# Tiles multiplied by x before its norm is known, and weight rests queued behind the norm's chain on VectorE

## The chip, the core and the metric

The kernel runs on one core of one Trainium2 chip. The metric is the device time of one execution in microseconds (us). Engines are named as the profile names them: PE is TensorE (PEld its weight loads), DVE VectorE, ACT ScalarE, POOL GpSimd and SP SyncE, whose queue issues most loads.

## What is computed

A trunk of two layers on 256 tokens of width 1024 (float32). Each layer is a mixer and a channel mixer, each behind a norm that is modulated by a conditioning vector c (adaLN):

```python
for l in range(DEPTH):
    mod = c_act @ w_ada[l] + b_ada[l]
    sh1, sc1, g1, sh2, sc2, g2 = split(mod)
    h = rmsnorm(x, ln1_g[l]) * (1.0 + sc1) + sh1
    x = x + g1 * mixer(h, ...)            # GLA branch + RWKV-7 branch, gated, then w_out
    h = rmsnorm(x, ln2_g[l]) * (1.0 + sc2) + sh2
    f = swiglu(h, w1, w3, w2) if l % 2 == 0 else moe(h, ...)   # (silu(h w1) * (h w3)) w2, or 8 experts, top 2
    x = x + g2 * f
return rmsnorm(x, lnf_g)
```

`rmsnorm(x, g)` is `x * rsqrt(mean(x*x) + 1e-6) * g`: one number for each token times a gain for each channel. Here channels lie on the partitions and tokens along the free dimension, so the norm is one row of 256 factors, the gain and the shift are one column each.

## The kernel before

All products are made from float32 values split in two: a high part (a rounded copy, written by ScalarE) and a rest (value minus copy, written by VectorE, `split`, L358 and L359). A **tile** (`project`, L374 to L385) is a 128-column piece of a weight with 8 blocks of 128 input channels; each block is three matmuls of 128x128 by 128x256 (high by high L382, high by activation's rest L383, weight's rest by high L384), so a tile is 24 products. The activations are `hh` and `hl`, both parts of the normalized input, which `norm_split` (L387 to L394) makes for each block: VectorE multiplies x by gain and norm (t, L391), ScalarE adds the shift and rounds (hh, L392), VectorE takes the rest (hl, L393).

The norm: ScalarE squares x (`stat`, L309), TensorE sums the squares over the channels (L318), VectorE takes the reciprocal root in a chain of eight tiny instructions (`rsq`, L331 to L338), TensorE spreads the two columns over all partitions (`spread`, L344).

The order of the program is: mixer 0, `ffn` (the dense feed-forward of layer 0, 22 blocks of two tiles and one second multiplication each, L1011 to L1013, then the x updates L1039), mixer 1 (first the tiles 0 and 1, whose `shift` is L571/L572, and the small projection `pap`, L585 to L587; L596 and L599 multiply the first tile's result), the experts (`moe`). Each mixer contains a substitution loop (L700/L702, 30 steps on VectorE), after which VectorE turns the result (L704 to L706: TW, TT) and TensorE takes it up (L711, L719), then four chunks (L732 to L767) follow one another.

Beside all this the adaLN weights of what comes next are multiplied: `feed` takes one 128x1024 piece (`araw`, loaded by POOL's queue, L230) and adds it into `aacc` on VectorE (L251 for the first of eight, L253 for the others); after eight pieces TensorE and VectorE finish the group (L267, L275, L278). `pace` calls `feed` once in a number of tiles, and two pieces at a time (six in the feed-forward) are loaded ahead.

The order of the instructions on PE, DVE and ACT is set by the framework's scheduler from the program; only SP's loads stand in an order written by hand in the mixers and the feed-forward. Each engine works its own queue in order.

## Time and profile before

| | |
|---|---|
| median of 3 runs | 1783.13 us (1782.68 to 1784.4) |
| the profiled execution | 1787.74 us |
| its span, first to last instruction | 1785.9 us |
| mean granted TensorE clock | 0.969 |
| busy: TensorE, VectorE, ScalarE | 1708.7, 1152.2, 830.1 us |
| HBM read | 517.84 MB, 291 GB/s over the span |

The places that the change touches lie at 369 to 391 us (mixer 0 to feed-forward), 566 to 600 us (feed-forward to mixer 1) and in mixer 1 up to its chunks (600 to 780 us); the experts run from about 910 us to the end. A busy TensorE is not TensorE at its peak: a product of 128x256 follows the one before it after 0.12 us at full clock. In the timelines the first column is the start in us, the second the duration, and what stands in brackets is the idle time before it with what ended it.

### The profile page before, as it was taken

Reading aid. Unit: us, or ns where it says so; the run is one execution under the profiler, and the core shown is the slowest. Engines: PE = TensorE matmul, PEld = TensorE weight load, DVE = VectorE, ACT = ScalarE, POOL = GpSimd, SP = SyncE. Lnnn points to the kernel's source line nnn. Section 1 sums busy time; section 2 is a strip of 40 time slices with the busy share of each in tenths; the row PEclk is TensorE's granted clock in tenths of the full one; section 3 lists DMA queues with packets and bytes.
Section 4 is the critical chain, followed back from the end, with each engine's and each line's share of the span. In section 5 each row is a group of like instructions: output and inputs, shape, how many; then the busy total and the mean of one; then the engine's idle time right before and its main releaser. Section 6 shows DMA issues by size and latency. Waiting matters only on the chain.

```text
span 1785.9 us, 29944 instructions
## 1 busy us (share of the span) xinstructions
PE 1708.7 (96%) x11887; PEld 1406.2 (79%) x11887; DVE 1152.2 (65%) x1747; ACT 830.1 (46%) x1194; POOL 57.3 (3%) x103
## 2 busy tenths in 40 slices
PE   7898999989999999899979999999999999999997
PEld 6787889989999888899977875678656886578754
DVE  3789668776665879566768961498407982289611
ACT  3643324444444643234537750477306771267501
POOL 0000000010000000000010000000000000000001
PEclk9899799999999899799979999999999999999999
DMA  8654246777764434325678989999999999999995
GB/s 342 210 184 166 97 135 241 259 263 261 266 229 153 146 140 137 123 72 189 265 288 328 346 310 421 420 421 421 418 420 421 420 421 417 421 421 420 420 421 215
DMA packets 79973, 520.92 MB, mean 292 GB/s; under 512 B 9521, under 2 KB 10161, under 8 KB 22353
## 3 DMA queue, kind: packets, MB, share of 16 engines
q1 hardware_dynamic: 67440, 476.14, 67.2%
q0 software_dynamic: 11232, 40.90, 7.0%
q8 instruction: 95, 1.56, 0.3%
q10 hardware_dynamic: 1152, 1.89, 0.3%
q14 instruction: 54, 0.43, 0.1%
HBM read 517.84 MB, written 1.05 MB: 291 GB/s over the span
## 4 chain that ended last, share of the span: by engine, by line
PE 75%; issue 12%; DVE 6%; DMA 4%; ACT 2%; POOL 0%; SPq 0%; POOLq 0%; DVEq 0%; ACTq 0%
PE pj L1316 11%; PE pj L382 6%; PE pj L383 6%; PE pj L384 6%; PE pj L1320 6%; PE pj L1321 6%; PE pj L1322 6%; PE pc L1335 5%; DMA araw<-wada 3%; PE pc L1338 3%; PE pc L1340 3%; PE pc L1339 3%; PE pg L1365 1%; DVE lo L359 1%; PE pg L1289 1%
## 5 line engine op out<-in xcount | busy, mean ns | idle before, releaser
L1100 DVE TENSOR_TENSOR lo<-raw,hi 128x1024 fp32r<-128x1024 f32 x330 | 395.5, 1221 | 85.9 <-ACT hi L1099 78.5
L1099 ACT ACTIVATE hi<-raw 128x1024 fp32r<-128x1024 f32 x330 | 347.5, 1059 | 126.8 <-PE pj L1321 82.1
L358 ACT ACTIVATE hi<-raw 128x1024 fp32r<-128x1024 f32 (+2 forms) x209 | 213.7, 1025 | 271.3 <-PE pj L383 200.1
L382 PE MATMUL pj<-hh,hi 128*128 128x256 f32 x1040 | 306.4, 296 | 5.5 <-DVE t L572 3.2
L384 PE MATMUL pj<-hh,lo 128*128 128x256 f32 x1040 | 303.0, 292 | 3.3 <-DVE lo L359 3.3
L359 DVE TENSOR_TENSOR lo<-raw,hi 128x1024 fp32r<-128x1024 f32 (+2 forms) x209 | 246.3, 1180 | 89.0 <-ACT hi L358 84.4
L383 PE MATMUL pj<-hl,hi 128*128 128x256 f32 x1040 | 302.3, 292 | 0.0
L382 PEld LDWEIGHTS pj<-hh,hi 128*128 128x128 f32 x1040 | 204.3, 197 | 13.8 <-issue 4.7
L384 PEld LDWEIGHTS pj<-hh,lo 128*128 128x128 f32 x1040 | 204.0, 196 | 5.6 <-DVE lo L359 3.9
L383 PEld LDWEIGHTS pj<-hl,hi 128*128 128x128 f32 x1040 | 203.8, 196 | 1.9 <-issue 0.3
L1316 PE MATMUL pj<-raw,xs 128*64 128x256 f32 x1792 | 201.3, 381 | 0.0
L1320 PE MATMUL pj<-hi,xh 128*128 128x512 f32 x448 | 181.5, 405 | 0.5 <-ACT hi L1099 0.5
L1322 PE MATMUL pj<-lo,xh 128*128 128x512 f32 x448 | 178.5, 398 | 1.9 <-DVE lo L1100 1.9
L1321 PE MATMUL pj<-hi,xl 128*128 128x512 f32 x448 | 177.8, 397 | 0.0
L1316 PEld LDWEIGHTS pj<-raw,xs 128*64 128x64 f32 x1792 | 125.8, 137 | 65.0 <-issue 4.7
L1360 DVE TENSOR_TENSOR late<-late,pj 128x512 f32<-128x512 f32 (+1 forms) x56 | 30.7, 549 | 207.5 <-PE pj L1316 201.0
L1322 PEld LDWEIGHTS pj<-lo,xh 128*128 128x128 f32 x448 | 84.5, 189 | 25.8 <-DVE lo L1100 5.3
L1335 PE MATMUL pc<-raw,as 128*64 128x512 f32 x448 | 102.2, 595 | 0.0
L1320 PEld LDWEIGHTS pj<-hi,xh 128*128 128x128 f32 x448 | 84.7, 189 | 21.3 <-ACT hi L1099 1.9
L1321 PEld LDWEIGHTS pj<-hi,xl 128*128 128x128 f32 x448 | 84.7, 189 | 18.7
L253 DVE SCALAR_TENSOR_TENSOR aacc<-araw,csg,aacc 128x1024 f32<-128x1024 f32 x70 | 89.6, 1280 | 12.6 <-DMA araw<-wada 11.8
L1338 PE MATMUL pc<-hi,acts 128*128 128x512 f32 x224 | 88.2, 394 | 0.0
(406 smaller groups left out, 2660.6 us busy)
## 6 DMA issues: line engine op xcount, KB each, us to landing
raw<-moe SPq DMA_DIRECT2D x333, 1024.0 KB, 18.2
raw<-win SPq DMA_DIRECT2D x43, 1024.0 KB, 5.0
araw<-wada POOLq DMA_DIRECT2D x78, 512.0 KB, 4.7
raw<-f SPq DMA_DIRECT2D x33, 1024.0 KB, 6.9
raw<-wv SPq DMA_DIRECT2D x8, 1024.0 KB, 4.9
raw<-wog SPq DMA_DIRECT2D x8, 1024.0 KB, 5.4
raw<-wad SPq DMA_DIRECT2D x6, 1024.0 KB, 8.1
raw<-wor SPq DMA_DIRECT2D x4, 1024.0 KB, 5.2
```

The lines of the kernel that those rows point to most:

```text
L358: nc.scalar.activation(hi[:, :w], src, AF.Copy)
L359: nc.vector.tensor_tensor(lo[:, :w], src, hi[:, :w].bitcast(F32), ALU.subtract)
L382: nc.tensor.matmul(o, hi[:, s], ah[:, kc, :], start=kc == 0, stop=False)
L383: nc.tensor.matmul(o, hi[:, s], al[:, kc, :], start=False, stop=False)
L384: nc.tensor.matmul(o, lo[:, s], ah[:, kc, :], start=False, stop=kc == nk - 1)
L1099: nc.scalar.activation(hi, w[:, s], AF.Copy)
L1100: eng.tensor_tensor(lo, w[:, s], hi.bitcast(F32), ALU.subtract)
L1316: nc.tensor.matmul(p[64 * n:64 * n + 64, :T], x[:, kc], hi[:, z * 512 + n * T:z * 512 + n * T + T], start=kc == 0, stop=kc == KC - 1)
L1320: nc.tensor.matmul(p, x[0][:, kc], hi[:, s], start=kc == 0, stop=False)
L1321: nc.tensor.matmul(p, x[1][:, kc], hi[:, s], start=False, stop=False)
L1322: nc.tensor.matmul(p, x[0][:, kc], lo[:, s], start=False, stop=kc == KC - 1)
L1335: nc.tensor.matmul(py[0][64 * n:64 * n + 64], act[:, a:a + CAP], hi[:, s], start=first, stop=last)
```

## The change

Four things change.

1. **Early tiles.** At the start of the feed-forward and of mixer 1 a new function `scaled` splits x times gain, without norm and shift, in two parts `xh` and `xl` (eight copies on ScalarE, eight rests on VectorE), and puts the shift behind them as two more columns. The first three tiles (`EARLY`) multiply 258 columns of it. What they give is then treated by `normed`: VectorE copies the added column out, multiplies the 256 others by the spread norm, and the column is added (in the silu's bias, in the product of the two halves, or by itself in mixer 1).
2. **The norm's row** is copied by ScalarE from PSUM to SBUF (`rs`), and `norm_split` reads it there.
3. **A fence.** `rstd` keeps the last instruction of the rsq chain; every weight rest and every `aacc` piece that the program writes after it is queued behind it on VectorE (`issue_after`).
4. **The end of the feed-forward.** The second multiplications of the last two blocks are made together at the end, in halves, each x update behind its last product.

```diff
+        with self.behind():
+            if kc == 0:
+                self.acc = self.st.tile([P, D], F32, name="aacc")
...
@@ rsq
-            nc.vector.scalar_tensor_tensor(y, t, a, y, ALU.add, ALU.mult)
+            last = nc.vector.scalar_tensor_tensor(y, t, a, y, ALU.add, ALU.mult)
+        self.chain = last.ins
@@ rstd
         y = self.rsq(self.ss[:, :2], 2, 1.0 / D, 1e-6)
+        self.fence = self.chain
...
+    def behind(self):
+
+        return self.tc.issue_after(self.fence) if self.fence else nullcontext()
@@ split
-        nc.vector.tensor_tensor(lo[:, :w], src, hi[:, :w].bitcast(F32), ALU.subtract)
+        with self.behind():
+            nc.vector.tensor_tensor(lo[:, :w], src, hi[:, :w].bitcast(F32), ALU.subtract)
@@ project
-        o = self.pj()[:, :T]
         ah, al = act
+        o = self.pj()[:, :ah.shape[-1]]
...
+    def scaled(self, gain, sh, xh, xl):
+
+        nc = self.nc
+        for d, op in ((xh, 0), (xl, 1)):
+            e = d[:, :, T:T + 2]
+            s = sh[:, :, None].to_broadcast([P, KC, 2])
+            if op:
+                nc.vector.tensor_tensor(e, s, xh[:, :, T:T + 2].bitcast(F32), ALU.subtract)
+            else:
+                nc.scalar.activation(e, s, AF.Copy)
+        for kc in range(KC):
+            g = gain[:, kc:kc + 1]
+            nc.scalar.activation(xh[:, kc, :T], self.x[:, kc, :], AF.Copy, scale=g)
+            nc.vector.scalar_tensor_tensor(xl[:, kc, :T], self.x[:, kc, :], g, xh[:, kc, :T].bitcast(F32), ALU.mult,
+                                           ALU.subtract)
+
+    def normed(self, ps, rs, tmp, col):
+
+        nc = self.nc
+        nc.vector.tensor_copy(col, ps[:, T:T + 1])
+        t = tmp()
+        nc.vector.tensor_tensor(t, ps[:, :T], rs, ALU.mult)
+        return t
...
+EARLY = 3
+LAST_F = 2
@@ mixer, l = 1
-        rs = k.rstd()
+        xh, xl = [dp.tile([P, KC, T + 2], F32R, name=n) for n in ("BK", "vt")]
+        k.scaled(gain, sh, xh, xl)
+        pre = {i: k.project(tile_of(i), (xh, xl)) for i in range(EARLY)}
+        rs = mis[:, :T]
+        nc.scalar.activation(rs, k.rstd(), AF.Copy)
         k.norm_split(range(KC), gain, sh, rs, hh, hl, t1)
@@ ffn
-        rs = k.rstd()
+        xh, xl = [dp.tile([P, KC, T + 2], F32R, name=n) for n in ("xh", "xl")]
+        k.scaled(gain, sh, xh, xl)
...
+        for i in range(EARLY):
+            pre[i] = k.project(load(i // 2)[:, i % 2 * 1024:i % 2 * 1024 + 1024], (xh, xl))
+        rs = dp.tile([P, T], F32, name="rs")
+        nc.scalar.activation(rs, k.rstd(), AF.Copy)
+        col = dp.tile([P, EARLY], F32, name="col")
         k.norm_split(range(KC), gain, sh, rs, hh, hl, t1)
...
+        k.need(l, 5)
+        ws = [k.split(w2) for _, _, w2 in pend]
+        for m0 in (0, 4):
+            each = [(p, w, m) for m in range(m0, m0 + 4) for p, w in zip(pend, ws)]
+            if m0 == 0:
+                each = [(p, w, m) for p, w in zip(pend, ws) for m in range(4)]
+            for p, w, m in each:
+                second(*p[:2], w, m)
+                if p is pend[-1]:
+                    o = acc[m // 2][:, (m % 2) * T:(m % 2) * T + T]
+                    nc.vector.scalar_tensor_tensor(k.x[:, m], o, k.mod[l][:, 40 + m:41 + m], k.x[:, m], ALU.mult, ALU.add)
```

How the scheduler puts it on the engines shows at three places. The first is VectorE at the start of the feed-forward, in the norm's chain. The kernel before (L331 to L338 is the chain, aacc the adaLN pieces, t the first step of `norm_split`):

```order
L331 TENSOR_SCALAR rsq<-pc 128x2
L253 SCALAR_TENSOR_TENSOR aacc<-araw,csg,aacc 128x1024
L334 TENSOR_SCALAR rsq<-rsq 128x2
L278 TENSOR_TENSOR mod_78<-ada,vec 128x8
L336 TENSOR_TENSOR rsq<-rsq 128x2
L337 SCALAR_TENSOR_TENSOR rsq<-rsq 128x2
L338 SCALAR_TENSOR_TENSOR rsq<-rsq 128x2
L336 TENSOR_TENSOR rsq<-rsq 128x2
L337 SCALAR_TENSOR_TENSOR rsq<-rsq 128x2
L253 SCALAR_TENSOR_TENSOR aacc<-araw,csg,aacc 128x1024
L338 SCALAR_TENSOR_TENSOR rsq<-rsq 128x2
L253 SCALAR_TENSOR_TENSOR aacc<-araw,csg,aacc 128x1024
```

The changed kernel at the same place (the chain is L332 to L339, xl the rest of x times gain, col the added column of an early tile):

```order
L332 TENSOR_SCALAR rsq<-pc 128x2
L335 TENSOR_SCALAR rsq<-rsq 128x2
L408 SCALAR_TENSOR_TENSOR xl<-x,gain_3849,xh 128x256 x4
L337 TENSOR_TENSOR rsq<-rsq 128x2
L408 SCALAR_TENSOR_TENSOR xl<-x,gain_3849,xh 128x256 x2
L338 SCALAR_TENSOR_TENSOR rsq<-rsq 128x2
L339 SCALAR_TENSOR_TENSOR rsq<-rsq 128x2
L337 TENSOR_TENSOR rsq<-rsq 128x2
L414 COPY col<-pj 128x1
L338 SCALAR_TENSOR_TENSOR rsq<-rsq 128x2
L339 SCALAR_TENSOR_TENSOR rsq<-rsq 128x2
L279 TENSOR_TENSOR mod_78<-ada,vec 128x8
```

The aacc pieces have gone behind the chain; six of the eight xl and the copy of the first tile's column now stand in it.

The second is TensorE a little later, around the fourth tile, the first one of the feed-forward that multiplies hh and hl in the change. The kernel before (pj_4024 is the fourth tile, pj_3994 the third, lo the weight's rest):

```order
L384 MATMUL pj_3994<-hh_3847,lo_3996 128x256
L382 MATMUL pj_4024<-hh_3847,hi_4025 128x256
L383 MATMUL pj_4024<-hl_3848,hi_4025 128x256
L384 MATMUL pj_4024<-hh_3847,lo_4026 128x256
L382 MATMUL pj_4024<-hh_3847,hi_4025 128x256
```

The changed kernel (pj_3945 is the third tile, pj_4056 the fourth, pj_4127 the fifth):

```order
L392 MATMUL pj_3945<-xh_3851,lo_3947 128x258
L390 MATMUL pj_4056<-hh_3847,hi_4057 128x256
L391 MATMUL pj_4056<-hl_3848,hi_4057 128x256
L390 MATMUL pj_4127<-hh_3847,hi_4128 128x256
L391 MATMUL pj_4127<-hl_3848,hi_4128 128x256
L392 MATMUL pj_4056<-hh_3847,lo_4058 128x256
L390 MATMUL pj_4056<-hh_3847,hi_4057 128x256
```

The tile before the fourth has become an early one; in both orders the third matmul of the fourth tile takes the weight's rest, and the tile's others stand behind it.

The third is VectorE at the end of mixer 1's substitution loop. The kernel before (zt and ff are the loop's two instructions, L704 turns its result):

```order
L253 SCALAR_TENSOR_TENSOR aacc<-araw,csg,aacc 128x1024
L700 TENSOR_TENSOR zt<-ff 64x84
L359 TENSOR_TENSOR lo<-raw,hi 128x1024
L702 TENSOR_TENSOR ff<-ff,zt 64x3x28
L253 SCALAR_TENSOR_TENSOR aacc<-araw,csg,aacc 128x1024
L700 TENSOR_TENSOR zt<-ff 64x58
L703 MEMSET ff 64x32
L359 TENSOR_TENSOR lo<-raw,hi 128x1024
L702 TENSOR_TENSOR ff<-ff,zt 64x2x29
L253 SCALAR_TENSOR_TENSOR aacc<-araw,csg,aacc 128x1024
```

and, up to the turn,

```order
L700 TENSOR_TENSOR zt<-ff 64x30
L359 TENSOR_TENSOR lo<-raw,hi 128x1024
L702 TENSOR_TENSOR ff<-ff,zt 64x30
L253 SCALAR_TENSOR_TENSOR aacc<-araw,csg,aacc 128x1024
L704 STREAM_TRANSPOSE TW<-ff 32x32x32
```

The changed kernel (L744 and L746 are the loop's two instructions, L748 the turn; dg belongs to the experts' router):

```order
L367 TENSOR_TENSOR lo<-raw,hi 128x1024
L744 TENSOR_TENSOR zt<-ff 64x84
L1738 TENSOR_SCALAR dg<-router,gain_9447 128x8
L746 TENSOR_TENSOR ff<-ff,zt 64x3x28
L744 TENSOR_TENSOR zt<-ff 64x58
L747 MEMSET ff 64x32
L746 TENSOR_TENSOR ff<-ff,zt 64x2x29
L744 TENSOR_TENSOR zt<-ff 64x30
L746 TENSOR_TENSOR ff<-ff,zt 64x30
L748 STREAM_TRANSPOSE TW<-ff 32x32x32
```

No aacc piece is left in the loop (six stood in it), and ten weight rests instead of 13; the pieces of that group stand before the loop. On TensorE 66 products that stood between the last L683 and L711 now come after L711.

## Rows read from the trace of the kernel before

**Rows 1.** Page, busy time of each engine (share of the span, instructions).

```profile
PE 1708.7 (96%) x11887; PEld 1406.2 (79%) x11887; DVE 1152.2 (65%) x1747; ACT 830.1 (46%) x1194; POOL 57.3 (3%) x103
```

**Rows 2.** Table of stretches around the two norms: busy us of each engine, clock, DMA.

```profile
core 0: us, PE busy (x) PEld busy (x) DVE busy (x) ACT busy (x) POOL busy (x), PEclk, DMA share, GB/s
369.20:374.60 5.40, 1.81 (x19) 1.07 (x17) 4.75 (x14) 0.80 (x2) 0.00 (x0) 0.97 0.61 235
374.60:381.20 6.60, 5.44 (x23) 5.02 (x24) 6.54 (x15) 3.63 (x8) 2.11 (x4) 0.51 0.68 210
...
540.00:566.00 26.00, 26.00 (x219) 26.00 (x218) 13.36 (x16) 11.27 (x15) 0.00 (x0) 1.00 0.24 82
...
576.00:589.60 13.60, 9.70 (x44) 9.04 (x45) 10.41 (x28) 4.86 (x12) 1.58 (x3) 0.51 0.55 187
```

**Rows 3.** Timeline of VectorE, start of the feed-forward.

```profile
370.19 0.75 DVE L251 TENSOR_SCALAR aacc<-araw,csg 128x1024 f32<-128x1024 f32 x1 [0.45 <-PE ada L267]
...
374.43 0.15 DVE L338 SCALAR_TENSOR_TENSOR rsq<-rsq 128x2 f32<-128x2 f32 x1
...
377.08 1.27 DVE L393 SCALAR_TENSOR_TENSOR hl<-t,mod,hh 128x256 fp32r<-128x256 f32 x3
...
386.05 1.23 DVE L359 TENSOR_TENSOR lo<-raw,hi 128x1024 fp32r<-128x1024 f32 x1
```

**Rows 4.** Timeline of TensorE, the same stretch.

```profile
374.64 1.22 PE L344 MATMUL pc<-cst,rsq 128*128 128x128 f32 x4 [3.51 <-DVE rsq L338]
376.98 0.80 PE L382 MATMUL pj<-hh,hi 128*128 128x256 f32 x2 [1.12 <-ACT hh L392]
...
390.50 0.28 PE L383 MATMUL pj<-hl,hi 128*128 128x256 f32 x1
390.62 0.28 PE L384 MATMUL pj<-hh,lo 128*128 128x256 f32 x1
390.75 0.28 PE L1011 MATMUL pc<-ah,hi 128*128 128x256 f32 x1
```

**Rows 5.** Timelines of VectorE and TensorE, feed-forward to mixer 1.

```profile
579.55 0.16 DVE L331 TENSOR_SCALAR rsq<-pc 128x2 f32<-128x2 f32 x1 [2.93 <-PE pc L318]
...
582.08 0.16 DVE L338 SCALAR_TENSOR_TENSOR rsq<-rsq 128x2 f32<-128x2 f32 x1
...
584.63 0.58 PE L382 MATMUL pj<-hh,hi 128*128 128x256 f32 x1 [1.11 <-ACT hh L392]
...
597.16 0.48 PE L596 MATMUL pc<-t,sm 64*128 64x256 f32 x1
```

**Rows 6.** Table of stretches in mixer 1, columns as in rows 2.

```profile
600.00:673.00 73.00, 71.34 (x523) 64.55 (x522) 59.36 (x117) 44.43 (x74) 0.70 (x2) 1.00 0.40 142
667.20:725.50 58.30, 53.80 (x391) 48.84 (x389) 55.12 (x103) 23.29 (x39) 2.64 (x5) 1.00 0.42 143
780.00:905.00 125.00, 124.72 (x1040) 122.59 (x1040) 86.14 (x174) 57.36 (x96) 0.00 (x0) 1.00 0.58 220
730.70:753.40 22.70, 22.70 (x233) 21.32 (x234) 10.89 (x12) 5.00 (x9) 0.00 (x0) 0.50 0.22 78
```

**Rows 7.** Groups by line, VectorE, loop of mixer 1: busy, mean ns, idle before.

```profile
L359 DVE TENSOR_TENSOR lo<-raw,hi 128x1024 fp32r<-128x1024 f32 x13 | 15.9, 1225 | 0.4
...
L253 DVE SCALAR_TENSOR_TENSOR aacc<-araw,csg,aacc 128x1024 f32<-128x1024 f32 x5 | 6.4, 1284 | 1.7 <-DMA araw<-wada 1.6
```

**Rows 8.** Chain of waits of mixer 1, and TensorE's timeline at its end.

```profile
667.19 1.30 DVE big L685 x2
...
721.37 5.98 DMA araw<-wada
727.38 1.29 DVE aacc L253
728.69 1.95 DVE TW L704
730.68 3.62 PE L711 MATMUL pc<-TW,big 32*32 32x32 f32 x64 [5.10 <-DVE TW L704]
```

**Rows 9.** TensorE's timeline and a stretch of the table, loop's end in layer 0.

```profile
196.48 0.71 PE L881 MATMUL pg<-att,vt 128*128 128x128 f32 x4 [1.02 <-DVE g L874]
199.18 1.65 PE L711 MATMUL pc<-TW,big 32*32 32x32 f32 x40 [1.98 <-DVE TW L704]
...
199.20:200.50 1.30, 1.30 (x38) 1.30 (x39) 1.30 (x1) 0.07 (x1) 0.00 (x0) 0.89 0.00 0
```

More of the change, by code (lines that the diff above doesn't have):

```diff
@@ L162, in __init__ @@
         self.ps = ctx.enter_context(tc.tile_pool(name="ps", bufs=1, space=PSUM))
-        self.side = self.wide = None
+        self.side = self.wide = self.fence = None
         self.late = []
@@ L248, in feed @@
         l, g, kc, w, _ = self.units.pop(0)
-        if kc == 0:
-            self.acc = self.st.tile([P, D], F32, name="aacc")
-            nc.vector.tensor_scalar(self.acc, w, self.sc[:, 0:1], None, ALU.mult)
-        else:
-            nc.vector.scalar_tensor_tensor(self.acc, w, self.sc[:, kc:kc + 1], self.acc, ALU.mult, ALU.add)
+        with self.behind():
+            if kc == 0:
+                self.acc = self.st.tile([P, D], F32, name="aacc")
+                nc.vector.tensor_scalar(self.acc, w, self.sc[:, 0:1], None, ALU.mult)
+            else:
+                nc.vector.scalar_tensor_tensor(self.acc, w, self.sc[:, kc:kc + 1], self.acc, ALU.mult, ALU.add)
         if kc == KC - 1:
@@ L385, in project @@
         return o
+    def scaled(self, gain, sh, xh, xl):
[5 more added lines that the diff above has]
+                nc.vector.tensor_tensor(e, s, xh[:, :, T:T + 2].bitcast(F32), ALU.subtract)
+            else:
+                nc.scalar.activation(e, s, AF.Copy)
[10 more added lines that the diff above has]
+        return t
     def norm_split(self, kcs, gain, sh, rs, hh, hl, tmp):
@@ L561, in mixer @@
         nc.scalar.activation(ta[:, GATE_SEQ[i - 14][1]], pre.pop(i), AF.Tanh, scale=0.5)
-    def tile_of(i):
-        w = unit(i // 2)
-        return w[:, (i % 2) * 1024:(i % 2) * 1024 + 1024]
     def proj(i):
-        return pre.pop(i) if i in pre else k.project(tile_of(i), act)
+        if i not in pre:
+            return k.project(tile_of(i), act)
+        if not l:
+            return pre.pop(i)
+        t = k.normed(pre.pop(i), rs, t1, zt[:, i:i + 1])
+        nc.vector.tensor_scalar(t, t, zt[:, i:i + 1], None, ALU.add)
+        return t
     def shift(ps, i):
@@ L999, in ffn, with load @@
         gain, sh = k.gain(l, 2)
-        rs = k.rstd()
+        xh, xl = [dp.tile([P, KC, T + 2], F32R, name=n) for n in ("xh", "xl")]
+        k.scaled(gain, sh, xh, xl)
+        w13, w2s = {}, {}
+        def load(f):
+            if f not in w13:
+                w13[f] = k.raw(A["f13"][f])
+                if f % 2 == 0:
+                    w2s[f // 2] = k.raw(A["f2"][f // 2], True)
+            return w13[f]
+        pre = {}
+        for i in range(EARLY):
[3 more added lines that the diff above has]
+        col = dp.tile([P, EARLY], F32, name="col")
         k.norm_split(range(KC), gain, sh, rs, hh, hl, t1)
@@ L1003, in ffn, with second, seconds, hidden @@
         pend = []
-        def second(f, a, w2):
+        def second(f, a, w, m):
             ah, al = a
-            hi, lo = k.split(w2)
-            for m in range(8):
-                o = acc[m // 2][:, (m % 2) * T:(m % 2) * T + T]
-                s = slice(m * P, m * P + P)
-                nc.tensor.matmul(o, hi[:, s], ah, start=f == 0 and m % 2 == 0, stop=False, skip_group_check=True)
-                nc.tensor.matmul(o, hi[:, s], al, start=False, stop=False, skip_group_check=True)
-                nc.tensor.matmul(o, lo[:, s], ah, start=False, stop=f == NF - 1, skip_group_check=True)
+            hi, lo = w
+            o = acc[m // 2][:, (m % 2) * T:(m % 2) * T + T]
+            s = slice(m * P, m * P + P)
+            nc.tensor.matmul(o, hi[:, s], ah, start=f == 0 and m % 2 == 0, stop=False, skip_group_check=True)
+            nc.tensor.matmul(o, hi[:, s], al, start=False, stop=False, skip_group_check=True)
+            nc.tensor.matmul(o, lo[:, s], ah, start=False, stop=f == NF - 1, skip_group_check=True)
+        def seconds(f, a, w2):
+            w = k.split(w2)
+            for m in range(8):
+                second(f, a, w, m)
+        def hidden(f):
+            ps = []
+            for i in (2 * f, 2 * f + 1):
+                w = load(f)[:, i % 2 * 1024:i % 2 * 1024 + 1024]
+                if i in pre:
+                    ps.append((k.normed(pre.pop(i), rs, t1, col[:, i:i + 1]), col[:, i:i + 1]))
+                else:
+                    ps.append((k.project(w, (hh, hl)), None))
+            (p1, b1), (p3, b3) = ps
+            u = t1()
+            nc.scalar.activation(u, p1, AF.Silu, **({} if b1 is None else {"bias": b1}))
+            if b3 is None:
+                nc.vector.tensor_tensor(u, u, p3, ALU.mult)
+            else:
+                nc.vector.scalar_tensor_tensor(u, p3, b3, u, ALU.add, ALU.mult)
+            ah = dp.tile([P, T], F32R, name="ah", bufs=LAST_F + 2)
+            al = dp.tile([P, T], F32R, name="al", bufs=LAST_F + 2)
+            nc.scalar.activation(ah, u, AF.Copy)
+            nc.vector.tensor_tensor(al, u, ah.bitcast(F32), ALU.subtract)
+            return f, (ah, al), w2s[f // 2][:, (f % 2) * 1024:(f % 2) * 1024 + 1024]
         for f in range(NF):
```

27 lines of the change are left out of this document (8 added, 19 removed).

## The prediction

> **What bounds the kernel now.** The page comes first: TensorE is busy 96% of the span [rows 1]. The table of stretches then says where it is not. Inside the feed-forward it never rests (26.00 of 26.00 us) and from 780 to 905 us it rests 0.28 us of 125 [rows 2, 6], so outside a few places the end moves by what TensorE has left to do and by its clock. Those places are the three that the change touches, and the timelines of VectorE and TensorE tell what ends each wait.
>
> Place A, from mixer 0 to the feed-forward. TensorE waits 3.51 us for the last step of the norm's chain (rsq, L338) and 1.12 us more for the first hh [rows 4]; the granted clock is 0.97 before and 0.51 from 374.6 to 381.2 us [rows 2], that is 1.2 instead of 2.4 GHz. But VectorE is no freer: busy 4.75 of 5.40 and 6.54 of 6.60 us [rows 2]. Place B, from the feed-forward to mixer 1: chain at 579.55 to 582.24 us, first product 584.63, the matmuls of L596 and L599, which wait for the first tile's shift, at 597.16 [rows 5]. Place C, the substitution loop of mixer 1 (L700/L702): VectorE carries it together with 13 weight rests and six pieces of aacc [rows 7]; the last piece waits for its DMA, and TensorE stands 5.10 us until TW is turned round [rows 8]. Then it runs 22.70 us without a gap at clock 0.50 [rows 6].
>
> **Place A, step by step.** In the change's order VectorE has in front of the fourth tile's rest lo (it starts at 386.05 and ends at 387.28 us before [rows 3]): eight xl at the price of an hl, 1.27/3 = 0.42 us [rows 3], 3.4 us; one strip and three columns at the price of an rsq step, 0.15 us [rows 3], 0.6 us; three products PSUM times rs, no row of this operand, taken as 0.42 us like hl, 1.3 us (bounds: 0.15, a small instruction, and 1.22, a whole rest). That is 5.3 us more. Three of the six aacc pieces that stood there now come later, 3 x 1.28 = 3.8 us less [rows 7]. So the rest ends at about 388.8 us, 389 with a short wait for tile 2's hi, which ScalarE now makes after the copy of rs. In TensorE's order 23 of the fourth tile's 24 products stand behind that rest; at 0.12 us, the step from 390.50 to 390.62 [rows 4], they end near 391.8 us, and the first block's second multiplication, at 390.75 before [rows 4], is **1.0 us later**. The 72 products of the early tiles do fill the old wait, but TensorE must then wait for VectorE, about 5 us up to 389 (by the same count tile 2's rest ends near 381.2 us, and its last 22 products follow to 384). After 3.51 us of waiting the clock was 0.51 until 4.2 us after the first product (376.98 to 381.2) [rows 2, 4]; the same again costs half of 4.2, **2.1 us**, where before that loss is already in the 390.75. A: **3.1 us slower**; bounds 0.2 slower (multiplications at 0.15, no fall of the clock; for a gain VectorE would need room, and there is none [rows 2]) and 6.7 slower (at 1.22, and the low clock over 6.6 us).
>
> **Place B.** The last two blocks' second multiplications, interleaved with the x updates, cost nothing: the same products in the same busy stretch. The gain is that 72 products go where TensorE waited; the price is the chain. The copy of tile 0's added column stands inside it on VectorE, so the chain can't end before tile 0 has: xh begins behind the last square, near 576.3 us, the first rest xl ends near 577.5, and 24 products at half clock [rows 2], 0.21 to 0.24 us each, end near 583; a weight rest, 1.23 us [rows 3], and the last two steps stand behind the copy, so the chain ends at about 584.9 instead of 582.24 [rows 5]. The spread matmuls stand behind tile 2 (about 588.4 us), so hh begins near 590, the small projection pap follows it hl by hl to about 596.7, and L596 comes at 598.9 instead of 597.16: 1.7 us later, with one 24-product tile already done that was not (2.9 us), less 0.6 us of waits behind it. B: **0.6 us faster**, bounds 2.7 slower (the whole delay of the chain) and 8 faster (the second rival).
>
> **From 600 us to the loop.** By the order twelve more aacc pieces stand here than before: four of the first group, pushed back from the norm's chain, and all eight of the second group, of which six stood in the loop: 0.75 [rows 3] + 11 x 1.28 = 14.8 us. VectorE has 73.00 - 59.36 = 13.6 us free [rows 6]. **1.2 us slower**; bounds 0, if TensorE doesn't need the time, and 2.8, with one more wait for a DMA like the 1.6 us in [rows 7].
>
> **Place C.** The loop loses those six pieces (6.4 + 0.75 us), the wait of 1.6 us and three of its 13 rests (3.7 us) [rows 7]: 12.5 of the 63.4 us from the last big (667.19) to the turned TW (728.69 + 1.95) [rows 8]. TensorE has 66 products fewer in front of L711 there, 7.9 us, which it does afterwards. Worth: 12.5 - 7.9 = **4.6 us faster**. Check: from 667.2 to 725.5 TensorE works 53.80 us [rows 6], so 45.9 now, in 50.9 us of VectorE: 5.0 us of idling instead of 9.6, and of it 1 to 3 us at L711 instead of 5.10. Bounds: 0 (the wait comes back somewhere else) and 9.6 (no idling left).
>
> **The clock at C** decides more than all of this. 22.70 us at 0.50 hold 11.35 us of full-clock work [rows 6], so keeping the clock up would be worth 11 us. In layer 0 the same code waits 1.02 and 1.98 us only, begins L711 at full clock, and then falls in it: 0.89 over 1.3 us [rows 9]. I take it that a wait of 1 to 3 us makes it fall again: 0 us. The Trainium skill, "TensorE: Matmul & The Clock Gate", section "What's actually happening", puts the half clock down to idleness and lets activity release it; taken alone, it lets the clock stay up when the long wait goes. By that the sum would be 11 us lower; layer 0 speaks against it [rows 9], so it is a rival.
>
> **Else.** On POOL the memset of TT now stands ahead of one aacc load; both buffers of that load are full then, so it costs nothing. SP's loads keep their order. In the experts the order is unchanged; they move with their start. Order and price of everything before 369 us are the same.
>
> **Sum.** 3.1 - 0.6 + 1.2 - 4.6 = 0.9 us faster, on 1787.74 us of the profiled execution (span 1785.9 and 1.8 around it): 1786.8. The median of the runs, 1783.13, is 4.6 below the profiled one: **1782.2 us**. A measurement of this kernel tells about 0.2%, 3.6 us, from no change.
>
> **Rivals.**
> 1. The clock stays up at C: 1782.2 - 11 = 1771. For it: the wait shrinks from 5.10 us, and the bounds reach 0. Against it: layer 0 [rows 9].
> 2. The norm at B is covered in full: the tiles run at full clock and the column copy waits for nothing. TensorE idles 13.60 - 9.70 = 3.9 us there and loses half of 9.70 to the clock [rows 2], 8.7 us at most instead of 0.6: 1774. For it: VectorE has air at B (10.41 of 13.60 us). Against it: the copy inside the chain. At A nothing is free for it.
> 3. Slower: the column copy holds VectorE's queue. If tile 0 ends later than VectorE reaches the copy, then the chain, the spread, hh and every rest behind the fence wait. Price: A's second multiplication at 394 instead of 391.8 and the low clock 6.6 us long (2.2 + 1.2), B at 2.7 slower instead of 0.6 faster (3.3): 1788.9. It decides from the point at which the copy waits over 2 us. That one waiting instruction holds all behind it is seen at 727.38 us: TW's turn needs nothing of the aacc piece and starts only after it [rows 8]. The Trainium skill states it as a rule of the strict order of VectorE's and ScalarE's queues ("TensorE: Matmul & The Clock Gate", section "Architectural detail"); the trace agrees with its 1.6 us.
> That the early tiles don't run early is excluded by the order.
>
> **How the numbers follow.** Forecast 0.46, with a range of its own from 1778 to 1787; rival 1 0.24; rival 2 0.08; rival 3 0.22. Faster by over 0.2%: rivals 1 and 2 and 0.08 of the forecast, 0.40. Slower: rival 3 and 0.07 of the forecast, 0.29. Within: 0.31. The range, 1769 to 1790, reaches to rivals 1 and 3 with some 2 us around them.
>
> **What would show it.** Right: idling of about 5 us on TensorE before the fourth tile's rest near 389 us and clock 0.5 after it; the second multiplication near 392; no aacc between the L700 and L702 of mixer 1; L711 waiting 1 to 3 us; clock 0.50 behind it. Wrong: L711 at clock 1.00 (rival 1); the feed-forward's first block ahead of 390 (my count of VectorE's work at A); the wait for TW back at 5 us; chains that end over 3 us later than before (rival 3).

## The result: 0.7% slower, outside the range

The changed kernel takes 1796.54 us (median of four runs, 1794.64 to 1799.68) against 1782.91 us (four runs, 1782.19 to 1784.4) for the kernel before: ratio **1.0070**, 95% interval 1.0055 to 1.0085. The forecast was 1782.2 us, with a range up to 1790. The profiled execution of the change took 1794.94 us (span 1793.1, mean clock 0.969). It came to the end of mixer 0 4.0 us earlier than that of before (last x update done at 365.7 against 369.7 us), in code that the change leaves alone (the fence is set there too, but VectorE, TensorE and ScalarE run the same instructions in the same order), so everything is counted from there: 1416.2 us to the end before, 1427.4 in the change, 11.2 longer.

TensorE's row on the page of the change, against the first of [rows 1]:

```profile
PE 1708.3 (95%) x11887; PEld 1403.1 (78%) x11887; DVE 1161.4 (65%) x1780; ACT 838.2 (47%) x1214; POOL 57.3 (3%) x103
```

TensorE is busy as long as before, so the added time is mostly waiting. Where it lies shows in the table of stretches, cut at the same events in both kernels: last x update of mixer 0, first second multiplication of the feed-forward, last x update there, L596 (L640 in the change), the loop's first step, L711 (L755), the chunks' last product of UV, the experts' first weight product. The kernel before:

```profile
core 0: us, PE busy (x) PEld busy (x) DVE busy (x) ACT busy (x) POOL busy (x), PEclk, DMA share, GB/s
369.70:390.80 21.10, 16.35 (x115) 15.09 (x108) 19.82 (x38) 10.49 (x18) 3.70 (x7) 0.84 0.62 211
...
575.10:597.20 22.10, 17.15 (x104) 15.60 (x103) 16.56 (x40) 9.12 (x22) 2.64 (x5) 0.69 0.55 177
597.20:673.10 75.90, 74.24 (x545) 67.09 (x545) 62.23 (x122) 47.13 (x78) 1.06 (x2) 1.00 0.40 139
673.10:730.70 57.60, 48.22 (x346) 43.38 (x344) 52.89 (x102) 22.39 (x37) 3.16 (x6) 0.99 0.50 171
730.70:772.50 41.80, 41.80 (x449) 37.93 (x449) 21.39 (x31) 10.49 (x19) 0.00 (x0) 0.73 0.20 68
772.50:926.00 153.50, 143.39 (x1188) 140.10 (x1188) 102.62 (x225) 67.47 (x115) 6.97 (x3) 0.95 0.59 227
```

The change:

```profile
365.70:390.20 24.50, 18.37 (x116) 17.00 (x109) 20.57 (x50) 13.38 (x25) 4.04 (x8) 0.81 0.71 265
...
574.40:602.70 28.30, 19.47 (x116) 16.99 (x115) 22.99 (x54) 13.09 (x29) 2.65 (x5) 0.70 0.38 130
602.70:687.00 84.30, 77.09 (x553) 69.23 (x552) 72.78 (x134) 49.03 (x83) 5.29 (x10) 0.96 0.53 181
687.00:732.30 45.30, 38.34 (x276) 34.67 (x277) 42.33 (x96) 16.32 (x28) 0.00 (x0) 1.00 0.33 113
732.30:771.30 39.00, 39.00 (x445) 33.69 (x445) 17.09 (x23) 11.21 (x18) 0.00 (x0) 0.82 0.17 59
771.30:932.10 160.80, 150.76 (x1233) 146.29 (x1233) 106.57 (x230) 70.92 (x121) 6.98 (x3) 0.95 0.52 197
```

Products have moved across these cuts, so durations alone mislead. What can be compared is TensorE's **lost time**: the idling (length less busy) and what the low clock takes (length times 1 less the clock). For place B of the change: 28.30 - 19.47 = 8.8, and 28.30 x 0.30 = 8.5, together 17.3 us.

| lost us | A | B | L596 to loop | loop | after the turn (L711 on) |
|---|---|---|---|---|---|
| before | 8.1 | 11.8 | 1.7 | 10.0 | 11.3 |
| the change | 10.8 | 17.3 | 10.6 | 7.0 | 7.0 |
| difference | +2.7 | +5.5 | +8.9 | -3.0 | -4.3 |
| forecast | +3.1 | -0.6 | +1.2 | -4.6 for both | |

They add up to 9.8 us; the rest of the 11.2 lies in the experts. Two steps failed: B, and the stretch up to the loop. TensorE's timeline there (the waits of over 1 us):

```profile
588.26 0.60 PE L346 MATMUL pc<-cst,rsq 128*128 128x128 f32 x4
597.48 0.37 PE L629 MATMUL pj<-hh,hi 128*16 128x256 f32 x1 [8.61 <-DVE t L416]
...
612.25 1.13 PE L643 MATMUL pc<-t,sm 64*128 64x256 f32 x4 [1.31 <-ACT t L656]
620.30 0.58 PE L390 MATMUL pj<-hh,hi 128*128 128x256 f32 x1 [4.13 <-DVE t L416]
629.83 0.39 PE L390 MATMUL pj<-hh,hi 128*128 128x256 f32 x1 [1.33 <-DVE t L616]
```

L629 is the first product of the small projection `pap`. It does not read what L416 writes: L416 (an early tile times the norm's row, in `normed`) empties the PSUM buffer that `pap` needs. There are three such buffers (`pj`), and the three early tiles hold all of them until L416 has multiplied them. The factor is not what is late: ScalarE has copied its row (L593) at 589.68 us. Below are this copy and then VectorE's timeline, which shows why the first L416 comes 7.2 us after it:

```profile
589.31 0.37 ACT L593 ACTIVATE mis<-pc 128x256 f32<-128x256 f32 x1
```

```profile
583.19 0.16 DVE L414 COPY zt<-pj 128x1 f32<-128x1 f32 x1 [2.18 <-PE pj L392]
...
584.60 0.16 DVE L339 SCALAR_TENSOR_TENSOR rsq<-rsq 128x2 f32<-128x2 f32 x1
...
590.17 1.28 DVE L254 SCALAR_TENSOR_TENSOR aacc<-araw,csg,aacc 128x1024 f32<-128x1024 f32 x1 [1.56 <-DMA araw<-wada]
591.38 1.27 DVE L423 SCALAR_TENSOR_TENSOR t<-x,gain,mis 128x256 f32<-128x256 f32 x3
...
596.92 0.41 DVE L416 TENSOR_TENSOR t<-pj,mis 128x256 f32<-128x256 f32 x1
...
608.46 1.28 DVE L254 SCALAR_TENSOR_TENSOR aacc<-araw,csg,aacc 128x1024 f32<-128x1024 f32 x1 [0.76 <-DMA araw<-wada]
...
614.13 1.28 DVE L254 SCALAR_TENSOR_TENSOR aacc<-araw,csg,aacc 128x1024 f32<-128x1024 f32 x1 [2.40 <-DMA araw<-wada]
...
619.85 0.40 DVE L416 TENSOR_TENSOR t<-pj,mis 128x256 f32<-128x256 f32 x1
```

The first L416 stands behind all eight t and six of the eight hl of `norm_split`, the third (619.85) behind nearly all of the decays' work (L649 to L659, made from the products of L640 and L643) and behind two aacc pieces that wait for their DMA. Its tile was finished before 588.46, so one PSUM buffer is blocked for 31 us. An order with L416 ahead of `norm_split` was not tried. After each of TensorE's long waits the clock is down as well (3.4 us lost to it between L640 and the loop).

### The profile page after: what moved, and what is told of

Same layout as the page of the kernel before. It is cut to its first block, busy times and chain, and to the rows that moved or that the text cites. A ratio compares the mean times of both kernels' runs of the same rounds, so it can differ in the third digit from the quotient of the medians.

```text
span 1793.1 us, 29996 instructions
## 1 busy us (share of the span) xinstructions
PE 1708.3 (95%) x11887; PEld 1403.1 (78%) x11887; DVE 1161.4 (65%) x1780; ACT 838.2 (47%) x1214; POOL 57.3 (3%) x103
## 3 DMA queue, kind: packets, MB, share of 16 engines
q8 instruction: 95, 1.56, 0.3%
## 4 chain that ended last, share of the span: by engine, by line
PE 77%; issue 8%; DVE 7%; DMA 5%; ACT 2%; POOL 0%; SPq 0%; DVEq 0%; POOLq 0%; ACTq 0%
PE pj L1397 11%; PE pj L390 7%; PE pj L391 7%; PE pj L392 7%; PE pc L1416 5%; PE pj L1401 5%; PE pj L1402 5%; PE pj L1403 5%; DMA araw<-wada 3%; PE pc L1419 3%; PE pc L1421 3%; PE pc L1420 3%; DVE lo L367 1%; PE pg L1446 1%; DMA raw<-moe 1%
## 5 line engine op out<-in xcount | busy, mean ns | idle before, releaser
L390 PE MATMUL pj<-hh,hi 128*128 128x256 f32 x992 | 291.8, 294 | 10.0 <-DVE t L416 6.4
L392 PE MATMUL pj<-hh,lo 128*128 128x256 f32 x992 | 288.7, 291 | 4.4 <-DVE lo L367 4.4
L391 PE MATMUL pj<-hl,hi 128*128 128x256 f32 x992 | 287.3, 290 | 0.0
L390 PEld LDWEIGHTS pj<-hh,hi 128*128 128x128 f32 x992 | 193.0, 195 | 17.8 <-issue 5.2
L392 PEld LDWEIGHTS pj<-hh,lo 128*128 128x128 f32 x992 | 192.9, 194 | 7.3 <-DVE lo L367 5.2
L391 PEld LDWEIGHTS pj<-hl,hi 128*128 128x128 f32 x992 | 192.9, 194 | 1.2
```

The costliest lines, as they stand in the source:

```text
L390: nc.tensor.matmul(o, hi[:, s], ah[:, kc, :], start=kc == 0, stop=False)
L391: nc.tensor.matmul(o, hi[:, s], al[:, kc, :], start=False, stop=False)
L392: nc.tensor.matmul(o, lo[:, s], ah[:, kc, :], start=False, stop=kc == nk - 1)
```

## The experiments

All runs were compared with the kernel before on the same chip; a ratio below 1 is faster. Lost time is worked out as above, from each run's own stretches (the clock is read to two digits, so 0.4 us is its grain).

| run | ratio (95%) | A | B | to loop | loop | after turn |
|---|---|---|---|---|---|---|
| before | 1 | 8.1 | 11.8 | 1.7 | 10.0 | 11.3 |
| the change | 1.0070 (1.0055 to 1.0085) | 10.8 | 17.3 | 10.6 | 7.0 | 7.0 |
| no_early | 1.0018 (1.0009 to 1.0028) | 6.1 | 9.0 | 9.8 | 7.5 | 11.6 |
| ffn_only | 1.0037 (1.0023 to 1.0050) | 10.8 | 8.6 | 13.5 | 7.5 | 11.1 |
| mix_only | 1.0048 (1.0031 to 1.0065) | | | | | |
| early2 | 1.0046 (1.0032 to 1.0060) | 12.5 | 10.8 | 10.5 | 7.5 | 11.6 |
| fence_only | 1.0029 (1.0019 to 1.0039) | 6.5 | 9.0 | 12.1 | 7.9 | 10.1 |
| tail_only | 1.0042 (1.0029 to 1.0056) | 8.2 | 20.0 | 4.2 | 10.4 | 11.4 |
| no_fence | 1.0051 (1.0038 to 1.0064) | 17.1 | 15.3 | 5.6 | 9.2 | 3.2 |
| copy_out | 1.0058 (1.0045 to 1.0070) | 11.6 | 7.2 | 20.6 | 6.4 | 9.8 |
| ffn_fence | 0.9983 (0.9972 to 0.9995) | 5.2 | 10.6 | 1.7 | 11.6 | 10.8 |
| hold | 0.9952 (0.9939 to 0.9965) | 5.3 | 9.6 | 0.1 | 8.3 | 10.1 |
| before_less | 1.0039 (1.0026 to 1.0052) | 8.2 | 13.9 | 8.6 | 7.2 | 10.4 |
| after_less | 1.0047 (1.0029 to 1.0065) | 10.8 | 15.3 | 11.0 | 7.2 | 10.4 |
| after_hold | 1.0013 (1.0003 to 1.0024) | 9.6 | 16.9 | 6.4 | 7.2 | 5.1 |
| out_hold | 1.0039 (1.0026 to 1.0052) | 11.3 | 7.6 | 17.4 | 6.4 | 5.1 |

The execution of mix_only that was profiled took 6859.86 us, its others 1789 to 1796 us, so no line of it is read.

### Which part of the change costs: early tiles left out, or fewer

no_early leaves the early tiles out in both places, ffn_only in mixer 1, mix_only in the feed-forward; the fence and the new end stay. early2 makes two.

```diff
# no_early (both places), ffn_only (mixer 1), mix_only (feed-forward); mixer 1's lines, the feed-forward's are like them
-        k.scaled(gain, sh, xh, xl)
-        pre = {i: k.project(tile_of(i), (xh, xl)) for i in range(EARLY)}
-        rs = mis[:, :T]
-        nc.scalar.activation(rs, k.rstd(), AF.Copy)
+        rs = k.rstd()
# early2
-EARLY = 3
+EARLY = 2
```

> The change without its early tiles: the fence and the new end of the feed-forward stay. Theory 1 (PSUM): the three early tiles hold all three buffers of pj until VectorE multiplies them by the norm, so TensorE has nowhere to write; without them 1780 to 1786 us, and no wait of TensorE for L416. Theory 2 (the fence): weight rests and aacc pieces pushed behind the chain pile up on VectorE and TensorE waits for that; the cost stays, 1789 us or more.

> Early tiles in the feed-forward alone. Theory 1: the feed-forward's own loss of some 3.5 us stays (the second multiplication 25 us behind the last x update instead of 21.5) and that of mixer 1 goes: 1784 to 1789 us. Theory 2: as without early tiles, 1789 us or more, the loss in mixer 1.

> Early tiles in mixer 1 alone. Theory 1: the waits of TensorE for L416 in mixer 1 (8.6 and 4.1 us) stay and with them most of the loss, 1789 to 1795 us. Theory 2: no better and no worse than without early tiles.

> Two early tiles instead of three, all else as in the change. Theory 1: one buffer of pj stays free, so the small projection starts with the first hh; the wait of 8.6 us falls under 3 us, and the time to 1785 to 1790 us. Theory 2: the fence and the chain are as before it, so 1793 us or more.

Without early tiles 0.5% of the 0.7% is gone. Neither theory's ranges held throughout: no_early (1787.1 us) and early2 (1792.7 us) fell between the two, ffn_only (1.0037, some 1791 us) into Theory 2's and mix_only into Theory 1's. At A they cost 4.7 us (6.1 against 10.8 in ffn_only), at B some 8 us (9.0 and 8.6 without, 17.3 with). Two tiles instead of three take the wait for L416 away at B (10.8 us) but not the loss up to the loop. And that loss is there without any early tile in mixer 1 (9.8 and 13.5 us): the PSUM buffers, which Theory 1 names, cannot be its only cause.

### Fence and end alone

fence_only is the kernel before with the fence, tail_only with the new end of the feed-forward; no_fence is the change with `behind` returning nothing; tail_only has that edit and no_early's.

```diff
# tail_only, no_fence
-        return self.tc.issue_after(self.fence) if self.fence else nullcontext()
+        return nullcontext()
```

> The kernel before with the fence alone. Without early tiles, fence and new end together cost 0.18% (3.2 us). Theory 2a (the fence costs it: aacc pieces that stood in gaps of the norm come later and collide): 1.0015 to 1.0025 of before. Theory 2b (the new end costs it): 0.9990 to 1.0005.

> The new end of the feed-forward alone, no fence, no early tiles. Theory 2a: 0.9985 to 1.0005 of before. Theory 2b: 1.0015 to 1.0025.

> The change without its fence: early tiles and new end stay, weight rests and aacc pieces may stand in the norm's chain. Theory 1 (PSUM): the buffers of pj are held as before, so the waits for L416 stay: 1.0045 or more. Theory 2a: the fence's 3 us come back, 1.0030 to 1.0055, if the chain is not held up longer by pieces that stand in it again.

The fence is two things. At A and B it saves 1.6 and 2.8 us; up to the loop it costs 10.4. (In the change, against no_fence, it saves 6.3 us at A, and costs 2.0 at B and 5.0 up to the loop.) TensorE's and VectorE's timelines of fence_only there (L580 is `shift`):

```profile
608.49 0.58 PE L390 MATMUL pj<-hh,hi 128*128 128x256 f32 x1 [4.97 <-DVE t L580]
```

```profile
590.51 1.28 DVE L254 SCALAR_TENSOR_TENSOR aacc<-araw,csg,aacc 128x1024 f32<-128x1024 f32 x1 [1.48 <-DMA araw<-wada]
...
597.33 1.28 DVE L254 SCALAR_TENSOR_TENSOR aacc<-araw,csg,aacc 128x1024 f32<-128x1024 f32 x1 [1.36 <-DMA araw<-wada]
...
637.41 1.28 DVE L254 SCALAR_TENSOR_TENSOR aacc<-araw,csg,aacc 128x1024 f32<-128x1024 f32 x1 [2.25 <-DMA araw<-wada]
```

Pushed back behind the chain, the first group's pieces come close together, and the second group's move from the loop to ahead of it. Each load takes about 5 us from issue to landing (next row: DMA issues of the change, KB each, median us to landing), and two are under way at a time, so VectorE stands at pieces whose data are not there, with the `shift` that TensorE needs behind them. Between 590 us and that `shift` (607.95 us) four pieces cost VectorE 2.8 us of waiting and 5.1 us of work.

```profile
araw<-wada POOLq DMA_DIRECT2D x78, 512.0 KB, 5.1
```

tail_only loses 8.2 us more at B than the kernel before: again a piece at the wrong place. Its VectorE and its TensorE:

```profile
585.42 1.28 DVE L254 SCALAR_TENSOR_TENSOR aacc<-araw,csg,aacc 128x1024 f32<-128x1024 f32 x1 [4.43 <-DMA araw<-wada]
```

```profile
587.70 0.79 PE L390 MATMUL pj<-hh,hi 128*128 128x256 f32 x2 [5.43 <-ACT hh L424]
```

The piece stands ahead of `norm_split`, and TensorE's wait for hh is the wait for that DMA. So the end's reordering is not free, as the forecast had it, where nothing keeps the pieces behind the chain; with the fence it is (no_early 9.0 at B, fence_only 9.0). tail_only (1.0042) lies outside what either theory allowed, fence_only (1.0029) a little above Theory 2a's range; with both of them the ratio is 1.0018 (no_early), so the parts do not add up.

### Early tiles copied out of PSUM

copy_out is the change with each early tile copied to SBUF by ScalarE when it is finished; the column copies on VectorE go.

```diff
+    def out(self, ps, pool):
+        o = pool.tile([P, T + 2], F32, name="out", bufs=EARLY)
+        self.nc.scalar.activation(o, ps, AF.Copy)
+        return o
...
-        nc.vector.tensor_copy(col, ps[:, T:T + 1])
...
-        pre = {i: k.project(tile_of(i), (xh, xl)) for i in range(EARLY)}
+        pre = {i: k.out(k.project(tile_of(i), (xh, xl)), dp) for i in range(EARLY)}
...
```

> The change, with ScalarE copying each early tile out of PSUM as soon as it ends; VectorE copies no column and multiplies out of SBUF. Theory 1: pj's buffers are free at once, TensorE's waits for L416 (8.6 and 4.1 us in mixer 1) fall under 3 us together, and most of mixer 1's loss of 0.3% goes: 1.0020 to 1.0045. The rival, that VectorE's work is the bound there: 1.006 or more, the waits only change their name.

```profile
591.40 0.29 PE L634 MATMUL pj<-hh,hi 128*16 128x256 f32 x1 [2.29 <-ACT hh L428]
...
621.07 1.08 PE L268 MATMUL ada<-aacc,cst 128*32 128x256 f32 x8 [9.85 <-DVE aacc L254]
```

At B the buffers were the main cause: `pap` begins 6.1 us earlier than in the change (591.40 against 597.48) and the loss falls from 17.3 to 7.2 us, the lowest of all runs. A part of this is the column copy, which the edit takes out of the chain: the chain ends 8.6 us behind the last x update instead of 10.4. But all of it returns before the loop: now TensorE's queue stands at the first group's product with aacc, 9.85 us, until VectorE has come to the last piece.

### Pieces kept where they were, or held behind the loop

ffn_fence is the kernel before with the fence, dropped at the start of mixer 1. hold is ffn_fence, and from there on the pieces of mixer 1 queue behind the turn of TW. The other two leave out seven additions of the first of the two groups that mixer 1 carries.

```diff
# ffn_fence and hold
         rs = k.rstd()
+        k.fence = None
# hold
-        with self.behind():
+        with self.behind(self.hold):
...
+    def behind(self, hold=None):
+        f = hold or self.fence
+        return self.tc.issue_after(f) if f else nullcontext()
...
-    nc.vector.transpose(TW[64:96].rearrange("p m s -> p s m"), Z[64:96].rearrange("p t s -> p s t"))
+    turned = nc.vector.transpose(TW[64:96].rearrange("p m s -> p s m"), Z[64:96].rearrange("p t s -> p s t"))
+    if l:
+        k.hold = turned.ins
# before_less and after_less
-        else:
+        elif (l, g) != (1, 4):
```

> The kernel before with the fence at the start of the feed-forward alone: weight rests and aacc pieces written behind the norm's chain queue behind it there, and the fence is dropped at the start of mixer 1, so mixer 1 has the order of the kernel before. Theory 3 (the fence helps at A and costs from 600 us on, by the second group of aacc pieces that comes ahead of the loop): from the last x update of mixer 0 to the first second multiplication 19.6 us as in fence_only, against 21.0 in the kernel before (1.4 us saved); from the first product of L596 to the loop's first step 76 us (not 90); L711's wait 5 us as before. In all 0.9985 to 1.0000. Rival (the time lost from 600 us on comes with the saved time itself, since the DMA of the pieces is what is late): 90 us there again, and 1.002 or more.

> As ffn_fence, and in mixer 1 the aacc pieces are queued behind the turn of TW, so that neither the stretch from L596 to the loop nor the loop carries them. Theory 3 (VectorE's work on the pieces in that stretch is what TensorE waits for): from L596 to the loop 72 to 76 us, the loop until L711 some 48 us instead of 57.6 (six pieces of 1.28 us and the wait of 1.6 us fewer), L711's wait 1 to 3.8 us, and behind it clock 0.5 to 0.7 again for some 8 to 20 us; the pieces fit into the time after the loop, where VectorE is busy under half. 0.992 to 0.998. Rival (the pieces come late for the group's end, which TensorE or VectorE then needs in the experts): the gain in mixer 1 is given back from 780 us on, 0.999 to 1.003.

> The kernel before without seven of the eight additions into aacc of the second group that mixer 1 carries (layer 1, fifth of six groups of the adaLN: only the first 128 channels of c are multiplied). Their loads stay. What the pieces cost the loop: six pieces of 1.28 us and the wait of 1.6 us there, 9 us of VectorE's, of which TensorE idles 5.1 us at L711. Theory 3: 2 to 5 us faster than the kernel before, up to 11 more if L711 then keeps the full clock: 0.990 to 0.999. Rival (the pieces lie beside other work): 0.9995 to 1.0005.

> The changed kernel without the same seven additions (layer 1, fifth of six groups of the adaLN: only the first 128 channels of c are multiplied; loads stay). Theory 3 (these pieces, now ahead of the loop, are what the 9.0 us lost from L596 to the loop are made of): the time lost there falls from 10.7 us to 4 or less, and the ratio from 1.007 to 1.002 to 1.004. Rival (the loss there comes from the three PSUM buffers and the early tiles' L416, not from the pieces): the lost time stays above 8 us and the ratio above 1.005.

ffn_fence keeps the fence's gain at A (5.2 us lost) and with mixer 1's old order loses 1.7 us up to the loop, as before (VectorE's order from L596 to the turn is the old one, instruction for instruction): what cost there was the fence in mixer 1, not the time that the fence had saved. hold then takes the pieces out of both stretches; it is the fastest of all kernels, 1777.22 us (median of six), 0.5% under before (0.3% of it by holding the pieces, the rest as in ffn_fence) and, by the two ratios, 1.2% under the change. Its stretches from L596 to the chunks, and VectorE behind the turn:

```profile
590.50:663.70 73.20, 73.13 (x531) 65.91 (x531) 60.50 (x118) 47.47 (x78) 0.00 (x0) 1.00 0.39 130
663.70:708.60 44.90, 40.18 (x286) 37.33 (x285) 40.22 (x90) 16.00 (x29) 0.00 (x0) 0.92 0.35 118
708.60:750.70 42.10, 42.08 (x427) 34.00 (x427) 22.82 (x29) 11.09 (x17) 2.65 (x5) 0.76 0.33 107
```

```profile
712.32 1.29 DVE L254 SCALAR_TENSOR_TENSOR aacc<-araw,csg,aacc 128x1024 f32<-128x1024 f32 x1
...
725.68 0.69 DVE L755 COPY UV<-pc 64x512 f32<-64x512 f32 x1 [10.54 <-PE pc L753]
```

TensorE rests 0.07 us of 73.20, the loop takes 44.9 us instead of 57.6, and VectorE idles 10.54 us behind the turn all the same, so the pieces have room there.

The two kernels with additions left out do not test what they were meant to. The group (1, 4) of the edit (layer 1, fifth group) is the first of mixer 1's two: the kernel before adds it from 570.12 to 602 us, and the six pieces in its loop belong to the next group. With the edit the group that begins at 567.40 us in before_less has one piece, and the next group begins here:

```profile
578.97 0.75 DVE L251 TENSOR_SCALAR aacc<-araw,csg 128x1024 f32<-128x1024 f32 x1 [0.86 <-PE ada L267]
```

The scheduler has moved all eight pieces of that group out of the loop and the time behind it, to between 579 and 615 us. Both kernels were expected to lose less and did not (8.6 us up to the loop in before_less, against 1.7); in before_less TensorE waits 3.0 us there for aacc ahead of the group's end. What the pieces in the loop are worth, hold shows and these two do not.

### The change with the pieces held

after_hold is the change with hold's second edit, out_hold the same on top of copy_out.

> The changed kernel with one edit: in mixer 1 the aacc pieces written behind the loop queue behind the turn of TW, as in hold. It takes out of VectorE's queue what stands between the norm's chain and the loop: the three pieces of the second group and their waits for the DMA ahead of the third tile's L416, and the rest up to the loop. Theory 4 (the loss from L596's twin to the loop is the waiting of VectorE's queue for the pieces' DMA, with L416 and the group's products on TensorE queued behind it): lost TensorE time from the small products L640 to the loop 10.7 us falls to 4 or less, the loop and L711 as in hold (45 us, 1.9 us of waiting), the loss from the last x update of the feed-forward to L640 stays at 14 to 17 us (L629 still waits 6 to 9 us for L416, since the three PSUM buffers are still held until the spread factor is there). In all 0.998 to 1.002. Rival (the three PSUM buffers alone make that loss): L390 waits some 4 us for the third tile's L416 again, lost time 8 us or more, 1.003 or more.

> The same with the early tiles copied out of PSUM by ScalarE as in copy_out, so that no PSUM buffer waits for the norm's factor. Theory 4 with the buffers as cause at the start of mixer 1: lost TensorE time there 7 us as in copy_out (after_hold: 14 to 17), from L640 to the loop 4 us or less (copy_out: 20.6, of which 9.85 was the group's product L268 waiting for the last piece), ratio some 0.004 to 0.006 below after_hold: 0.993 to 0.998. Rival (whatever is gained at the start comes back in front of the loop, since VectorE's other work is the bound): lost time from L640 to the loop above 8 us, ratio within 0.002 of after_hold.

TensorE's timeline of after_hold, and its stretch up to the loop:

```profile
595.72 0.37 PE L630 MATMUL pj<-hh,hi 128*16 128x256 f32 x1 [8.64 <-DVE t L417]
...
612.25 0.38 PE L391 MATMUL pj<-hh,hi 128*128 128x256 f32 x1 [0.30 <-DVE t L417]
...
622.90 0.39 PE L391 MATMUL pj<-hh,hi 128*128 128x256 f32 x1 [2.30 <-DVE t L617]
```

```profile
600.50:678.40 77.90, 74.61 (x519) 67.13 (x519) 59.91 (x120) 46.93 (x78) 0.11 (x1) 0.96 0.34 115
```

With one edit 0.6 of the 0.7% are gone. The third tile's wait falls from 4.13 to 0.30 us, and the loss up to the loop from 10.6 to 6.4 us: less than the 10.7 to 4 that Theory 4 expected, but well off its rival. B stays at 16.9 us with a wait of 8.64 us, as expected for held buffers. The pieces ahead of the third L416 in the change belong to the first group, not to the second as the expectation has it; the edit holds the last four of the first group back as well. It takes their work and their waiting away together and does not tell the two apart.

out_hold goes its rival's way and further: B falls to 7.6 us, 17.4 us are lost up to the loop, and the ratio lies 0.0026 above that of after_hold, where the rival had it within 0.002. TensorE there, and the stretch that holds most of it:

```profile
615.81 0.58 PE L391 MATMUL pj<-hh,hi 128*128 128x256 f32 x1 [5.53 <-DVE t L622]
```

```profile
606.00:612.00 6.00, 3.71 (x15) 2.33 (x14) 5.66 (x16) 5.69 (x15) 0.00 (x0) 0.97 0.67 244
612.00:618.00 6.00, 2.19 (x10) 2.19 (x11) 4.31 (x13) 5.97 (x12) 0.00 (x0) 0.50 0.01 3
```

TensorE rests while VectorE (5.66 of 6.00 us) and then ScalarE (5.97) are full of the decays' work, that of both branches; the next `shift` stands behind it. As far as these rows show, early tiles make TensorE reach that work sooner, and it cannot go faster. B and the stretch behind it together lose 13.5 us before, 23.3 in after_hold, 25.0 in out_hold, 9.7 in hold without early tiles. The run hold also lacks the new end and, in mixer 1, the fence on the weight rests; no_early with the pieces held was not run, so what of the difference is due to the early tiles alone is not shown.

## Why the prediction was wrong, step by step

**A: right.** The loss grew by 2.7 us, forecast 3.1. VectorE was as full as counted: the fourth tile's rest is there 19.6 us behind the last x update (385.36 against 365.73 us), where the forecast had 19.3 (389 against 369.7). The waits are four of 0.96 to 1.91 us instead of one of about 5 us, as TensorE's timeline of the change shows, and the longest is already one for L416, so for a PSUM buffer. The first second multiplication stands 24.5 us behind the last x update instead of 21.1. By its own sign (near 392 us) the forecast had it at 22.3: the loss to the clock fell ahead of it (0.50 from 386 to 390.2 us) and not behind, which leaves the sum as it is.

```profile
374.78 0.39 PE L390 MATMUL pj<-xh,hi 128*128 128x258 f32 x1 [1.42 <-ACT hi L365]
376.76 0.39 PE L392 MATMUL pj<-xh,lo 128*128 128x258 f32 x1 [1.48 <-DVE lo L367]
...
383.92 0.36 PE L390 MATMUL pj<-hh,hi 128*128 128x256 f32 x1 [1.91 <-DVE t L416]
385.36 0.58 PE L392 MATMUL pj<-hh,lo 128*128 128x256 f32 x1 [0.96 <-DVE lo L367]
```

**B: wrong, 0.6 us faster forecast, 5.5 slower measured.** The chain was right: forecast to end near 584.9 us, its last step starts at 584.60; the spread forecast about 588.4, it is at 588.26 (the change reached mixer 1 0.7 us earlier than the kernel before, so counted from the last x update both are some 0.6 us later than forecast). The step that failed is "so hh begins near 590, the small projection pap follows it hl by hl to about 596.7". hh came some 1.7 us later by the pieces' DMA (`norm_split` starts at 591.38, its factor is there at 589.68), and `pap` waited for a PSUM buffer until 597.48. I counted who makes the data and not who holds the place they go to, so the sum had no term for the buffers; copy_out, where the early tiles hold none (and the chain is 1.8 us shorter), loses 10 us less there. The bound of 2.7 us "slower" took the chain's delay for the worst case.

**Up to the loop: mis-sized, 1.2 us forecast, 8.9 measured.** The twelve pieces were named, but weighed as busy time against free time (14.8 against 13.6 us). That step failed: the free time was no place to put them. In the change VectorE still idles 84.30 - 72.78 = 11.5 us of that stretch, while TensorE waits for what stands behind the pieces. To their work they add waits at the head of VectorE's queue, 0.76 + 2.40 us here and 1.56 at B, and after TensorE's own waits its clock is down. [Rows 7] and [rows 8] had shown a piece waiting 1.6 us for a DMA of 5.98, with TW's turn behind it. after_hold puts the pieces' share at 4.2 of the 8.9 us; of the rest out_hold suggests that it goes with the early tiles' lead, which VectorE and ScalarE take back.

**Place C: the right sign, larger.** From the last big (681.14 us) to the turned TW (730.25 + 1.97) it is 51.1 us, where the forecast had 50.9 of VectorE's work; before it was 63.4. These are the chain of the change, then TensorE's timeline, then its stretches:

```profile
681.14 1.30 DVE big L729 x2
...
730.25 1.97 DVE TW L748
```

```profile
732.26 3.40 PE L755 MATMUL pc<-TW,big 32*32 32x32 f32 x64 [3.79 <-DVE TW L748]
```

```profile
734.00:738.00 4.00, 4.00 (x38) 3.45 (x36) 3.17 (x3) 2.23 (x3) 0.00 (x0) 0.50 0.00 0
738.00:742.00 4.00, 4.00 (x71) 2.94 (x69) 1.17 (x1) 1.18 (x2) 0.00 (x0) 0.82 0.46 131
742.00:746.00 4.00, 4.00 (x29) 3.04 (x30) 0.00 (x0) 1.19 (x2) 0.00 (x0) 0.60 0.33 135
```

L711's wait became 3.79 us, a little over the 1 to 3 forecast, and the clock fell again, as forecast; but it came up sooner and lost 7.0 instead of 11.3 us, which the forecast had at no change. Of the loop itself 3.0 us were gained where the forecast had 4.6; that the whole came out larger is the clock's 4.3 us, and luck. Rival 1 (the clock stays up) did not happen, in this or any other run that was read.

**The new end: not free by itself** (tail_only), but hidden in this change by the fence.

**Rivals.** Rival 3 had the right mechanism, a waiting instruction that holds VectorE's queue, and mostly the wrong instruction. By its own signs it was met at B: the column copy waited 2.18 us, and the chain ended 10.4 us behind the last x update, 3.3 later than before. But the forecast had reckoned with nearly all of that (584.9), and most of what was lost beyond it came from the held buffers and from the pieces, whose work and DMA held what came after. The rule that it cited from the Trainium skill ("TensorE: Matmul & The Clock Gate", section "Architectural detail"), that VectorE's queue is worked strictly in order, agrees with the rows here: 4.43 us of waiting for a DMA in tail_only are 5.43 us of TensorE waiting for an hh that needs nothing of that piece. Rival 2 fell with B.

What stays open: how the loss up to the loop that after_hold still has (6.4 against 1.7 us) splits between the early tiles' extra work on VectorE, the new end, the fence on the weight rests and the order; and what decides how long the clock stays down after the turn.
